# Sixteen of the up projection's column pairs in seven block products instead of fourteen, one block's split through an accumulating DMA, and smaller raw loads

## The chip, the core and the metric

The kernel runs on one NeuronCore of a Trainium2 chip. The metric is device time in microseconds of one execution. A core has a matrix engine (TensorE; the profile lists its multiplications as PE and its weight loads as PEld), three engines for elementwise work (VectorE as DVE, ScalarE as ACT, GpSimd as POOL) and SyncE (SP), which here only starts DMAs. Each engine works off its own queue in order and waits on semaphores for the others. Operands lie in SBUF, products land in PSUM.

## The reference, cut to what matters

One encoder layer on 512 positions of width 1024, all in float32. The change lies in its feed-forward part alone:

```python
h = rmsnorm(x, ffn_pre_norm[l])
up = causal_dwconv(h @ w_ffn_up[l], ffn_conv_w[l], ffn_conv_b[l])
f_gate, f_val = jnp.split(up, 2, axis=-1)
f = (jax.nn.gelu(f_gate, approximate=True) * f_val) @ w_ffn_down[l]
x = x + rmsnorm(f, ffn_post_norm[l])
```

`w_ffn_up` is 1024 x 6144: 3072 gate columns and 3072 value columns. Before it stand an SSD mixer and an RG-LRU mixer with their projections, after it the down projection; both stay as they are.

## The kernel before, in words

**Two-part operands.** Every float32 operand of a large product is split in two parts, `hi` (a cast by ACT) and `lo` (the source minus `hi`, by DVE), and each product is three matmuls: hi by hi, hi by lo, lo by hi.

**Pairs.** The up projection works on 24 pairs `n` (`NF`), each of 128 gate columns and the 128 value columns that belong to them. A pair's weights are a 2 x 2 grid of blocks `a11`, `a12`, `a21`, `a22`: the first digit is gate (1) or value (2), the second is the half of the 1024 rows; each block is 128 partitions x 512 numbers, 256 KB. Pairs 0 and 1 go whole (`up_product`). The others, from `PLAIN` = 2, go through the loop near the end of the kernel, which walks over the *slots* of a pair: one slot is one block's product.

**Eight or seven.** `eight(n, old)` (L1050) multiplies all four blocks with all 512 positions: 4 slots of 12 matmuls over 512 columns. `seven(n, old)` (L1018) splits the positions in halves too and uses a Strassen-like scheme with sums of blocks `s1` to `s4` and of activations: 6 slots in `ORDER` = a11, s2, s4, s3, a12, s1, each 12 matmuls over 256 columns (`block_product`), and a seventh product, `a22` by the fourth activation sum, which is left to the next pair (`last_product(old)`). `seven_of[n]` says which; of pairs 4 to 23, every third is an eight, which makes 14 sevens and 6 eights; pairs 2 and 3 are eights too.

**What else a pair does.** `gate_part(old)` and `value_part(old)` are the causal convolutions of the pair before (one ACT pass and two DVE passes each, L226), `gelu_part(old)` the GELU by ACT; `value_part` ends with gate times value (L866). A seven adds its products on DVE: L1031 and L1044 to L1046 in its own slots, L1005 in `value_part` once `last_product` is through. L1046 reads the half bank into which `last_product` goes on to accumulate, so `last_product` has to wait for it; the product of `a12` has to wait for L1031 likewise.

**Splits ahead.** At the end of each slot `w_split` (L955) splits the block that is used five slots later. ACT writes `hi`, DVE `lo` (L952). For a seven it also makes `s2` = `s1` + `a11` (L965, in the turn of a11) and `s4` = `s2` + `a12` (L968, in the turn of s2); with `s3` it splits `a22` as well, into a tile that the profile calls `a`. For an eight it splits a11 with a12 and a21 with a22, 1024 wide.

**Loads.** `pair_load(n + 2)` in slot 0 of pair n has SP load the whole 1 MB of pair n + 2 into one of two buffers (called `H` in the profile, L926). It must wait until pair n's blocks have been read. `pair_sums(n + 2)` then loads the first term of `s1` and of `s3` (L940, SP) and adds the second by an accumulating DMA from POOL (L942), into tiles called `raw` and `third`.

**Order.** PE and ACT keep the order in which the program is written (`InOrder`). The order of DVE, of SP and of POOL is set by the framework's scheduler when the program is built.

Of the kernel before, what the change touches and what calls it, by code (L numbers as in the profile page):

```python
# [8 lines left out]
F32 = mybir.dt.float32  # L9
# [3 lines left out]
ALU = mybir.AluOpType  # L13

P = 128
D = 1024
# [6 lines left out]
NF = FF // P  # L23
EPS = 1e-6
DT_SLAB = 1
UP_SLAB = 77
# [30 lines left out]
def block_kernel(ctx: ExitStack, tc, x, slabs, wgate, pc, rows, out):  # L57
    nc = tc.nc
    V, A, PE = (InOrder(tc, e) for e in (nc.vector, nc.scalar, nc.tensor))
    G = nc.gpsimd  # L60
# [9 lines left out]
    def ps():  # L70
        return psum.tile([P, S], F32, tag="ps", name="ps")
# [16 lines left out]
    def mm3(acc, lhi, llo, rhi, rlo, start, stop):  # L88
        mm(acc, lhi, rhi, start, False)
        mm(acc, lhi, rlo, False, False)  # L90
        mm(acc, llo, rhi, False, stop)
# [57 lines left out]
    def load_slab():  # L149
        i = stream["load"]  # L150
        if i < end[0]:
            raws[i] = wts.tile([P, D], F32, tag="raw", name="raw")
            nc.sync.dma_start(out=raws[i], in_=slabs[i])
            stream["load"] += 1
# [707 lines left out]
    def f_gate(gt):  # L862
        A.activation(gt, gt, AF.Gelu_apprx_tanh)
# [26 lines left out]
    def h_split(m):  # L890
        t = lru8(F32R).rearrange("p k (two t) -> p k two t", two=2)
        comb[m] = t[:, :, 0, :], t[:, :, 1, :]
        split(*comb[m], tsum[m])
# [4 lines left out]
    def block_product(out, w, b, start=False):  # L898

        for k in range(HK):  # L900
            c = slice(k * P, (k + 1) * P)
            for e, (u, v) in enumerate(((0, 0), (0, 1), (1, 0))):
                PE.matmul(out, lhsT=w[u][:, c], rhs=b[v][:, k, :], start=start and k == e == 0,
                          stop=k == HK - 1 and e == 2, skip_group_check=not start)

    seven_of = [False] * 4 + [i % 3 != 2 for i in range(NF - 4)] + [False]
    ORDER = "a11", "s2", "s4", "s3", "a12", "s1"
    blocks = [(n, q) for n in range(PLAIN, NF + 1)  # L910
              for q in (ORDER if seven_of[n] else ("a11", "a12", "a21", "a22"))]
# [3 lines left out]
    blk, room, spare = {}, {}, []  # L915
# [3 lines left out]
    def drawn(n, i, h):  # L919
        return slabs[UP_SLAB + 2 * n + i, :, h * S:(h + 1) * S]  # L920

    def pair_load(n):
        if n > NF:
            return
        raw = pairs[:, n % 2, :]
        nc.sync.dma_start(out=raw.rearrange("p (i c) -> p i c", i=2),  # L926
                          in_=slabs[UP_SLAB + 2 * n:UP_SLAB + 2 * n + 2].rearrange("i p c -> p i c"))
        blk[n] = {q: raw[:, e * S:(e + 1) * S] for e, q in enumerate(("a11", "a12", "a21", "a22"))}
        blk[n]["raw"] = raw

    def pair_sums(n):

        if n > NF or not seven_of[n]:
            return
        b, i = blk[n], turn_of[n]
        b["s1"] = place("raw", i % 3 - 1) if i % 3 else third
        b["s3"] = place("raw", 2 + i % 2)
        adds = ("s1", (1, 0), (1, 1)), ("s3", (0, 0), (1, 0))
        for q, one, two in adds:
            nc.sync.dma_start(out=b[q], in_=drawn(n, *one))  # L940
        for q, one, two in adds:
            G.dma_start(out=b[q], in_=drawn(n, *two), accum_op=ALU.add)  # L942

    def place(kind, i):

        key = kind, i // 2
        if key not in room:
            room[key] = wts.tile([P, D], F32 if kind == "raw" else F32R, tag=kind, name=kind)
        return room[key][:, i % 2 * S:(i % 2 + 1) * S]

    def low(lo, src, hi):
        V.tensor_sub(lo, src, hi.bitcast(F32))  # L952

    def w_split(g):

        if g >= len(blocks):
            return
        n, q = blocks[g]
        b, i = blk[n], g % RING
        both = [place(kind, i) for kind in ("whi", "wlo")]  # L960
        b["w" + q] = both
        if seven_of[n]:
            if q == "a11":
                b["s2"] = place("raw", 4)
                V.tensor_add(b["s2"], b["s1"], b["a11"])  # L965
            elif q == "s2":
                b["s4"] = place("raw", 5)
                V.tensor_add(b["s4"], b["s2"], b["a12"])  # L968
            A.copy(both[0], b[q])
            low(both[1], b[q], both[0])  # L970
            if q == "s3":
                if not spare:
                    spare.append(work.tile([P, 2, 2, S], F32R, tag="M", name="a22", bufs=1))
                b["wa22"] = [spare[0][:, n % 2, e, :] for e in range(2)]
                A.copy(b["wa22"][0], b["a22"])
                low(b["wa22"][1], b["a22"], b["wa22"][0])
        elif q in ("a12", "a22"):
            hi, lo = (room[kind, i // 2] for kind in ("whi", "wlo"))
            src = b["raw"][:, 0:D] if q == "a12" else b["raw"][:, D:2 * D]
            A.copy(hi, src)  # L980
            low(lo, src, hi)
            if n == NF:
                splits[DOWN_SLAB + (q == "a22")] = hi, lo
# [7 lines left out]
    def gate_part(n):  # L991
        p = pr[n]
        p["g"] = conv(p["oa"], pcs[:, C_FCW + 3 * n:C_FCW + 3 * n + 3], C_FCB + n, 3)

    def gelu_part(n):
        f_gate(pr[n]["g"])

    def last_product(n):
        if seven_of[n]:
            block_product(pr[n]["z"][:, T1], blk[n]["wa22"], comb[3])  # L1000

    def value_part(n):
        p = pr.pop(n)
        if seven_of[n]:
            V.tensor_add(p["ob"][:, T0], p["u2"], p["z"][:, T1])  # L1005
            w = negw[:, 3 * n:3 * n + 3]
        else:
            w = pcs[:, C_FCW + 3 * (NF + n):C_FCW + 3 * (NF + n) + 3]
        vt = conv(p["ob"], w, C_FCB + NF + n, 3)
        f_done(n, p["g"], vt)  # L1010
# [38 lines left out]
    def eight(n, old):  # L1049
        p = pr.setdefault(n, {})  # L1050
        for e, o in enumerate(("oa", "ob")):
            p[o] = acc = ps()
            for h in range(2):
                w = blk[n]["wa%d%d" % (e + 1, h + 1)]
                for k in range(HK):
                    c = slice(k * P, (k + 1) * P)
                    mm3(acc, w[0][:, c], w[1][:, c], h2T[0][:, HK * h + k, :],
                        h2T[1][:, HK * h + k, :], h == k == 0, h == 1 and k == HK - 1)
                if old:
                    if e == h == 0:  # L1060
                        gate_part(old)
                    elif e == 0:
                        gelu_part(old)
                        last_product(old)
                    elif h == 0:
                        value_part(old)
                yield

# [15 lines left out]
    def f_split(i):  # L1084
        split(*f_parts(i), f_tile(i))


    for i in range(PLAIN):
        acc = up_product()
        if i == 0:  # L1090
            pair_load(PLAIN)
            pair_load(PLAIN + 1)
        gt = conv(acc, pcs[:, C_FCW + 3 * i:C_FCW + 3 * i + 3], C_FCB + i, 3)
        if i == 0:
            w_split(0)
            w_split(1)
            for m in range(4):
                h_sum(m)
        else:
            for g in range(2, RING - 1):  # L1100
                w_split(g)
            h_split(1)
            h_split(2)
        acc = up_product()
        vt = conv(acc, pcs[:, C_FCW + 3 * (NF + i):C_FCW + 3 * (NF + i) + 3], C_FCB + NF + i, 3)
        f_gate(gt)
        f_done(i, gt, vt)
# [3 lines left out]
    for n in range(PLAIN, NF):  # L1111
        for slot, _ in enumerate((seven if seven_of[n] else eight)(n, old)):
            w_split(g + RING - 1)
            g += 1
            if slot == 0:
                pair_load(n + 2)
                pair_sums(n + 2)
            if n == PLAIN and slot in (1, 2):
                h_split(3 * (slot - 1))
            if n < NF - 1:  # L1120
                continue
            if slot == 2:
                stream.update(load=DOWN_SLAB + 2, split=DOWN_SLAB + 2, use=DOWN_SLAB)
                end[0] = slabs.shape[0]
                load_slab()
            elif slot == 3:
                f_split(0)
                f_split(1)
            elif slot == 5:
                f_split(2)  # L1130
                f_split(3)
        old = n
# [100 lines left out]
```

## Time and profile before

| | us |
|---|---|
| median of 3 runs | 880.71 (878.99 to 883.2) |
| profiled execution, own time | 882.06 |
| its span, first to last instruction | 880.4 |
| PE busy in the span | 864.7 (98%) |
| DVE busy | 587.4 (67%) |
| ACT busy | 433.6 (49%) |
| POOL busy | 28.4 (3%) |
| granted TensorE clock, mean | 0.996 |

1.66 us of the profiled execution's time lie outside its span. "Busy" counts time in which an instruction of the engine was under way; instructions of one engine overlap at their ends, so what an instruction costs its queue is the distance between the start of one and the next, and not its duration. A line such as `[0.85 <-DVE tmp L1046]` says that the engine stood idle for 0.85 us before that instruction and that it was released by DVE's instruction of line 1046.

### The profile page before, as it was taken

Reading aid. Unit: us, or ns where it says so; the run is one execution under the profiler, and the core shown is the slowest. Engines: PE = TensorE matmul, PEld = TensorE weight load, DVE = VectorE, ACT = ScalarE, POOL = GpSimd, SP = SyncE. Lnnn points to the kernel's source line nnn. Section 1 sums busy time; section 2 is a strip of 40 time slices with the busy share of each in tenths; the row PEclk is TensorE's granted clock in tenths of the full one; section 3 lists DMA queues with packets and bytes.
Section 4 is the critical chain, followed back from the end, with each engine's and each line's share of the span. In section 5 each row is a group of like instructions: output and inputs, shape, how many; then the busy total and the mean of one; then the engine's idle time right before and its main releaser. Section 6 shows DMA issues by size and latency. Waiting matters only on the chain.

```text
span 880.4 us, 11591 instructions
## 1 busy us (share of the span) xinstructions
PE 864.7 (98%) x4554; PEld 739.7 (84%) x4554; DVE 587.4 (67%) x909; ACT 433.6 (49%) x714; POOL 28.4 (3%) x44
## 2 busy tenths in 40 slices
PE   7999999999999999999999999999999999999996
PEld 6888887888878888888888989889999899888885
DVE  6777657987875553444466797878978898743225
ACT  6444545578574443322365565445545556633222
POOL 0000000000000000000000101011011000000000
PEclk9999999999999999999999999999999999999999
DMA  6242223222334422222251837466556543422212
GB/s 225 96 146 96 96 94 110 90 84 79 119 103 174 154 96 96 87 99 101 97 191 25 212 127 195 126 180 170 165 144 181 156 127 113 144 96 95 96 48 96
DMA packets 36007, 108.47 MB, mean 123 GB/s; under 512 B 3632, under 2 KB 6896, under 8 KB 35440
## 3 DMA queue, kind: packets, MB, share of 16 engines
q1 hardware_dynamic: 30864, 99.34, 32.7%
q0 software_dynamic: 5088, 8.39, 5.7%
q8 instruction: 35, 0.57, 0.2%
q14 instruction: 20, 0.16, 0.1%
HBM read 103.49 MB, written 2.13 MB: 120 GB/s over the span
## 4 chain that ended last, share of the span: by engine, by line
PE 75%; DVE 11%; DMA 7%; ACT 5%; issue 2%; SPq 0%; DVEq 0%; ACTq 0%
PE ps L53 75%; DMA H<-slabs 5%; DVE wlo L952 2%; DVE tmp L226 2%; ACT whi L53 1%; DVE wlo L183 1%; ACT L L53 1%; DVE L L644 1%; DMA raw<-slabs 1%; ACT tmp L53 1%; DVE tmp L662 1%; DVE raw L965 0%; DMA wg<-wgate 0%; DVE L L638 0%; ACT junk L247 0%
## 5 line engine op out<-in xcount | busy, mean ns | idle before, releaser
L53 PE MATMUL ps<-H,whi 128*128 128x512 f32 x720 | 224.8, 395 | 0.4 <-DVE H L53 0.4
L183 DVE TENSOR_TENSOR wlo<-raw,whi 128x1024 fp32r<-128x1024 f32 x93 | 113.6, 1223 | 117.3 <-ACT whi L53 115.0
L53 ACT CAST whi<-raw 128x1024 fp32r<-128x1024 f32 (+1 forms) x144 | 127.5, 891 | 100.2 <-PE ps L53 96.6
L53 PE MATMUL ps<-C,whi 128*128 128x256 f32 (+1 forms) x656 | 166.5, 335 | 0.1
L53 PEld LDWEIGHTS ps<-H,whi 128*128 128x128 f32 x720 | 134.3, 188 | 30.3 <-issue 2.4
L53 PE MATMUL ps<-H,wlo 128*128 128x512 f32 x352 | 137.5, 391 | 0.4 <-DVE wlo L183 0.4
L53 PEld LDWEIGHTS ps<-C,whi 128*128 128x128 f32 x656 | 112.0, 190 | 12.6 <-DVE quad L1031 0.3
L53 PE MATMUL ps<-C,wlo 128*128 128x512 f32 (+1 forms) x360 | 122.2, 339 | 0.0
L53 PE MATMUL ps<-L,whi 128*128 128x256 f32 (+1 forms) x400 | 87.2, 300 | 0.0
L53 PE MATMUL ps<-whi,H 128*128 128x512 f32 x256 | 81.5, 394 | 0.0
L226 DVE SCALAR_TENSOR_TENSOR tmp<-ps,pcs,tmp 128x511 f32<-128x511 f32 (+2 forms) x100 | 74.5, 745 | 8.1 <-ACT tmp L53 7.2
L53 PEld LDWEIGHTS ps<-H,wlo 128*128 128x128 f32 x352 | 66.2, 188 | 15.3 <-DVE wlo L183 1.2
L53 PEld LDWEIGHTS ps<-C,wlo 128*128 128x128 f32 x360 | 68.3, 190 | 7.6
L53 PEld LDWEIGHTS ps<-L,whi 128*128 128x128 f32 x400 | 64.4, 191 | 2.5
L53 PEld LDWEIGHTS ps<-whi,H 128*128 128x128 f32 x256 | 48.1, 188 | 10.4 <-issue 0.5
L53 ACT ACTIVATE tmp<-tmp 128x512 f32<-128x512 f32 x36 | 22.7, 632 | 55.3 <-DVE tmp L226 55.3
L53 PE MATMUL ps<-wlo,H 128*128 128x512 f32 x128 | 49.8, 389 | 0.0
L952 DVE TENSOR_TENSOR wlo<-H,whi 128x512 fp32r<-128x512 f32 (+1 forms) x46 | 41.1, 894 | 9.7 <-ACT whi L53 9.6
L53 PE MATMUL ps<-L,wlo 128*128 128x256 f32 x168 | 47.5, 283 | 0.0
L53 ACT ACTIVATE tmp<-ps,halfb 128x512 f32<-128x512 f32 x32 | 21.5, 687 | 49.6 <-PE ps L53 49.6
L53 ACT ACTIVATE tmp<-ps,pcs 128x512 f32<-128x512 f32 x40 | 31.0, 776 | 27.9 <-PE ps L53 27.9
L53 PE MATMUL ps<-Y,whi 128*128 128x512 f32 x128 | 40.5, 397 | 0.2 <-DVE Y L200 0.2
(207 smaller groups left out, 1315.3 us busy)
## 6 DMA issues: line engine op xcount, KB each, us to landing
raw<-slabs SPq DMA_DIRECT2D x103, 512.0 KB, 3.2
H<-slabs SPq DMA_DIRECT2D x23, 1024.0 KB, 5.4
raw<-slabs SPq DMA_DIRECT2D x23, 256.0 KB, 3.8
raw<-slabs POOLq DMA_DIRECT2D x23, 256.0 KB, 6.5
quad<-x SPq DMA_DIRECT2D x8, 512.0 KB, 4.2
M<-acsD SPq DMA_DIRECT2D x4, 1024.0 KB, 4.6
out<-tmp SPq DMA_DIRECT2D x8, 256.0 KB, 2.0
third<-slabs SPq DMA_DIRECT2D x5, 256.0 KB, 6.3
```

The costliest lines, as they stand in the source:

```text
L53: return lambda *args, **kw: self.tc.keep_in_program_order(op(*args, **kw))
L183: V.tensor_sub(*late.pop(0))
L226: V.scalar_tensor_tensor(out=t[:, d:], in0=acc[:, :S - d], scalar=w[:, taps - 1 - d:taps - d], in1=t[:, d:], op0=ALU.mult, op1=ALU.add)
L644: V.tensor_tensor_scan(out=qq[:, e, :], data0=aa[:, e, :], data1=uu[:, e, :], initial=0.0, op0=ALU.mult, op1=ALU.add)
L662: V.tensor_mul(gl, gl, hs[i // 4][:, i % 4, :])
L952: V.tensor_sub(lo, src, hi.bitcast(F32))
```

## The change

More pairs go as sevens: 16 of pairs 4 to 23, with eights at 7, 12, 17 and 22, so that up to four sevens follow each other where it was two. The raw load is cut: of a seven, a11 and a12 come first (512 KB), then the terms of the sums, then a22 alone (256 KB); a21 is no longer loaded raw, and a22 takes the place of a21 or a22 in turn, so that it does not fall on the place that the pair two before it used. An eight's load comes in two halves. `s2` and `s4` are each made one turn later, just ahead of their own split. The low part of a22 is no longer made by DVE: ACT writes -hi into it, and a DMA from POOL adds a22. And in an eight, `last_product(old)` and `value_part(old)` move one slot back.

```diff
-    seven_of = [False] * 4 + [i % 3 != 2 for i in range(NF - 4)] + [False]
+    seven_of = [False] * 4 + [i % 5 != 3 for i in range(NF - 4)] + [False]
@@ pair_load
-        nc.sync.dma_start(out=raw.rearrange("p (i c) -> p i c", i=2),
-                          in_=slabs[UP_SLAB + 2 * n:UP_SLAB + 2 * n + 2].rearrange("i p c -> p i c"))
+        nc.sync.dma_start(out=raw[:, 0:D], in_=slabs[UP_SLAB + 2 * n])
         blk[n] = {q: raw[:, e * S:(e + 1) * S] for e, q in enumerate(("a11", "a12", "a21", "a22"))}
         blk[n]["raw"] = raw
+        if seven_of[n]:
+            blk[n]["a22"] = blk[n][("a21", "a22")[n // 2 % 2]]
+            pair_sums(n)
+            nc.sync.dma_start(out=blk[n]["a22"], in_=drawn(n, 1, 1))
+        else:
+            nc.sync.dma_start(out=raw[:, D:], in_=slabs[UP_SLAB + 2 * n + 1])
@@ w_split
-            if q == "a11":
+            if q == "s2":
                 b["s2"] = place("raw", 4)
                 V.tensor_add(b["s2"], b["s1"], b["a11"])
-            elif q == "s2":
+            elif q == "s4":
                 b["s4"] = place("raw", 5)
                 V.tensor_add(b["s4"], b["s2"], b["a12"])
             A.copy(both[0], b[q])
@@ w_split, with s3
-                A.copy(b["wa22"][0], b["a22"])
-                low(b["wa22"][1], b["a22"], b["wa22"][0])
+
+                hi, lo = b["wa22"]
+                A.copy(hi, b["a22"])
+                A.mul(lo, hi.bitcast(F32), -1.0)
+                G.dma_start(out=lo.bitcast(F32), in_=b["a22"], accum_op=ALU.add)
@@ eight
                     elif e == 0:
                         gelu_part(old)
+                    elif h == 0:
                         last_product(old)
-                    elif h == 0:
+                    else:
                         value_part(old)
@@ the loop over pairs, slot 0
                 pair_load(n + 2)
-                pair_sums(n + 2)
```

## Rows read from the trace of the kernel before

**Rows 1.** Page, part 1: busy time, share of the span and instructions of each engine

```profile
PE 864.7 (98%) x4554; PEld 739.7 (84%) x4554; DVE 587.4 (67%) x909; ACT 433.6 (49%) x714; POOL 28.4 (3%) x44
```

**Rows 2.** Page, part 4: chain that ended last, by engine

```profile
PE 75%; DVE 11%; DMA 7%; ACT 5%; issue 2%; SPq 0%; DVEq 0%; ACTq 0%
```

**Rows 3.** Busy time by stretch, pairs 6 to 23; each stretch starts with a matmul

```profile
core 0: us, PE busy (x) PEld busy (x) DVE busy (x) ACT busy (x) POOL busy (x), PEclk, DMA share, GB/s
550.55:564.04 13.49, 12.64 (x62) 10.38 (x61) 10.41 (x18) 4.70 (x10) 0.85 (x1) 1.00 0.37 104
...
615.49:627.85 12.36, 12.36 (x62) 10.45 (x61) 11.59 (x20) 7.66 (x13) 0.84 (x1) 1.00 0.54 141
...
691.53:710.25 18.72, 18.72 (x158) 18.71 (x157) 16.41 (x29) 10.34 (x20) 2.58 (x3) 1.00 0.71 194
...
sum 190.75, PE 187.88 PEld 174.77 DVE 162.32 ACT 100.58 POOL 17.06; mean PE 15.66 PEld 14.56 DVE 13.53 ACT 8.38 POOL 1.42
```

**Rows 4.** Waits of PEld, 531 to 742: us in total, times, longest

```profile
PEld ps L53 <- DVE tmp L1046: 4.4, 4, 1.5
PEld ps L53 <- DVE quad L1031: 0.3, 1, 0.3
```

**Rows 5.** Timeline of PE inside pair 6, an eight: start, us, instructions, idle before

```profile
555.79 0.39 PE L53 MATMUL ps<-C,wlo 128*128 128x512 f32 x1
557.03 1.70 PE L53 MATMUL ps<-L,a 128*128 128x256 f32 x12 [0.85 <-DVE tmp L1046]
```

**Rows 6.** Waits of DVE, 531 to 742

```profile
DVE raw L965 <- DMA H<-slabs: 14.8, 9, 2.7
DVE wlo L952 <- ACT whi L53: 12.3, 15, 1.4
```

**Rows 7.** Timeline of DVE where seven 19 ends and seven 20 begins

```profile
699.77 0.68 DVE L952 TENSOR_TENSOR wlo<-raw,whi 128x512 fp32r<-128x512 f32 x1
700.37 0.75 DVE L226 SCALAR_TENSOR_TENSOR tmp<-ps,pcs,tmp 128x510 f32<-128x510 f32 x1
701.03 0.68 DVE L952 TENSOR_TENSOR a<-H,a 128x512 fp32r<-128x512 f32 x1
701.63 0.69 DVE L866 TENSOR_TENSOR Y<-tmp 128x512 f32<-128x512 f32 x1
702.23 0.42 DVE L1044 TENSOR_TENSOR quad<-quad,ps 128x256 f32<-128x256 f32 x1
702.57 0.69 DVE L952 TENSOR_TENSOR wlo<-H,whi 128x512 fp32r<-128x512 f32 x1
...
703.50 0.42 DVE L1046 TENSOR_TENSOR tmp<-ps,quad 128x256 f32<-128x256 f32 x1
704.53 0.75 DVE L226 SCALAR_TENSOR_TENSOR tmp<-tmp,pcs 128x511 f32<-128x511 f32 x1 [0.61 <-ACT tmp L53]
```

**Rows 8.** Timeline of DVE around the start of pair 15, an eight

```profile
643.50 1.22 DVE L952 TENSOR_TENSOR wlo<-H,whi 128x1024 fp32r<-128x1024 f32 x1 [1.36 <-ACT whi L53]
644.65 0.41 DVE L1005 TENSOR_TENSOR tmp<-quad,ps 128x256 f32<-128x256 f32 x1
646.57 0.69 DVE L965 TENSOR_TENSOR raw<-raw,H 128x512 f32<-128x512 f32 x1 [1.51 <-DMA H<-slabs]
```

**Rows 9.** Page, part 6: DMA issues, count, KB each, median us to landing

```profile
raw<-slabs SPq DMA_DIRECT2D x103, 512.0 KB, 3.2
H<-slabs SPq DMA_DIRECT2D x23, 1024.0 KB, 5.4
...
raw<-slabs POOLq DMA_DIRECT2D x23, 256.0 KB, 6.5
```

**Rows 10.** Timeline of ACT in the same stretch as rows 7

```profile
699.48 0.62 ACT L53 CAST a<-H 128x512 fp32r<-128x512 f32 x1
700.00 0.36 ACT L53 COPY tmp<-ps 128x256 f32<-128x256 f32 x1
```

**Rows 11.** Groups by line on POOL, 550 to 742: busy us, mean ns | idle before

```profile
L942 POOL DMA_DIRECT2D raw<-slabs x17 | 14.5, 872 | 122.2 <-DMA raw<-slabs 121.4 <-issue 0.7
```

## The prediction

> **What bounds the kernel now.** I read the page's busy times first: PE is busy for 98% of the span, the next engine, DVE, for 67% [rows 1]. The chain that ended last agrees: 75% of it is PE, 11% DVE, 7% DMA [rows 2]. So time can only be won by giving PE less to do, or by closing the gaps in which it waits. The change touches the up projection's pairs alone, so I cut that stage into stretches of an eight, or of the sevens between two eights [rows 3]. Two kinds come out clean. An eight with the left-over product of the seven before it takes 12.36 us with PE busy throughout. Two sevens (13 products, since the last one is left over) take 18.72 us, or 1.44 us a product, 0.120 us a matmul. The eight alone is thus 12.36 - 1.44 = 10.92 us (0.2275 us a matmul), a seven is 7 x 1.44 = 10.08 us. The clock stands at 1.00 in all stretches, the upper of its two levels, 2.4 GHz.
>
> Six eights and six couples would take 6 x 12.36 + 6 x 18.72 = 186.48 us; they took 190.75 [rows 3]. The difference, **4.27 us, is all that PE loses in these pairs**. The waits say where: weight loads waited 4.4 us in four places for L1046 and 0.3 us for L1031 [rows 4]. The timeline shows one of the four: in eight 6, after the first half of its products, PE stands for 0.85 us until DVE is through with L1046, and the left-over product can start [rows 5].
>
> Why is DVE late there? It is not only busy; it waits: 14.8 us for raw loads at L965 and 12.3 us for ACT's casts at L952 [rows 6]. At L965 it stands 1.51 us in one instance, with L1044 to L1046 queued behind it [rows 8].
>
> **Part 1, two eights become sevens.** PE saves 2 x (10.92 - 10.08) = **1.68 us** [rows 3], on the path, since PE is the path. By the row a matmul costs its columns at 2.4 GHz and about 13 ns more (0.120 against 0.1067, 0.2275 against 0.2133). The Trainium skill (TensorE: Matmul & The Clock Gate, Wait — 56ns, not 53.3ns?) gives only about 2.5 ns more per matmul; by that the two pairs would save 2.4 us (estimate), but here 13 ns is measured, and a seven has 84 matmuls against 48, so the row decides.
>
> **Part 2, what DVE has to do.** Distances between starts are the cost: 0.60 us for a 512-wide subtraction, 0.66 for a convolution pass, 0.34 for a 256-wide addition [rows 7], 1.15 for a 1024-wide subtraction [rows 8]. A seven before: six block splits 3.60, a22 0.60, s2 and s4 1.20, four convolution passes 2.64, five additions 1.70, the last product 0.60: 10.34 us, more than the 10.08 that PE takes. After: 9.74. An eight: 2 x 1.15 + 2.64 + 0.60 = 5.54 of 10.92. Over pairs 4 to 23 DVE has 14 x 10.34 + 6 x 5.54 = 178.0 us before and 16 x 9.74 + 4 x 5.54 = 178.0 after: no change in sum, but it no longer falls behind by work alone while sevens follow each other. This is worth nothing in itself; it is what the next parts live on.
>
> **Part 3, last product one slot later in an eight.** L1046 had 5.46 us after the seven's end (half the eight, 10.92 / 2); it gets three quarters, 8.19 us. The longest of these waits was 1.5 us [rows 4], so 2.73 us more covers all four. Gain: up to 4.4 us of the waits; counted in the gap total, at most 4.27. The place where it can come back: `value_part` moves with it, so L1005, the last two passes and L866 (0.34 + 1.32 + 0.60 = 2.26 us of DVE) come 2.73 us later and end in the next seven's first slots, where L1031 must be done before the product of a12, 5.76 us in. That wait is at 0.3 us already [rows 4].
>
> **Part 4, smaller loads, s2 and s4 a turn later.** H landed in 5.4 us, 512 KB pieces in 3.2 [rows 9]; the addition s2 is due one slot (1.44 us) later. Together 3.6 us of slack against waits of at most 2.7 us [rows 6]: I expect nearly all of the 14.8 us of DVE idle time at L965 to go. PE gets none of that directly; it is DVE's lateness that shrinks. The price: ACT's cast of s2 now follows s2's addition directly, then comes the `lo` on DVE. The trace of before has no such chain. Lower bound 0, if the scheduler puts other DVE work between; upper bound two ACT casts of 0.52 us [rows 10] per seven, during which DVE stands. I take 0.2 us, nearer to 0, since DVE has some ten other instructions a pair to put there.
>
> **Part 5, a22's low part by DMA.** ACT gains one more pass of 0.52 us per seven [rows 10]; it is busy 10.34 of 18.72 us [rows 3], so that hides; if ACT were full, it would be 16 x 0.52 = 8.3 us. POOL gets a third issue per seven, 0.87 us [rows 11]; it is idle nearly always. Landing takes 6.5 us like the other accumulating DMAs [rows 9]. Cast, pass, issue and landing are 0.52 + 0.52 + 0.87 + 6.5 = 8.4 us from slot 4 of the pair before; the product is due after slot 3 of the pair after, in sevens 1.44 + 10.08 + 4 x 1.44 = 17.3 us later. The margin of 8.9 us can be lost behind a sum whose load is late on POOL's queue, where this DMA then stands too; I count 0, and rival C has the other end. The bytes moved per seven are the same 2 MB, at a DMA share of 0.71 [rows 3], so transfers stay hidden.
>
> **Part 6, four sevens in a row.** A seven then has 9.74 us of work, 0.61 us of waiting for ACT's convolution pass [rows 7] and 0.2 from part 4: 10.55 us against 10.08. So DVE falls behind by about 0.5 us per seven. At the end of the first of a run L1046 was through at 703.92 [rows 7], 3.75 us after the seven's end at 691.53 + 6 x 1.44 = 700.17 [rows 3]; the fourth would be at 5.2 us, under the 5.76 that a seven leaves and the 8.19 that an eight leaves. L1031 is tighter. I put 1.2 us for the stage (three runs of four, 0.2 us in the third and fourth); bounds 0 and 4.27, the gap total of now.
>
> **Sum.** 1.68 + 4.27 - 1.2 = **4.75 us** off the profiled execution's 882.06 (880.4 of span and 1.66 around it): 877.31. The median of the runs shown is 1.35 us below that execution, so 880.71 - 4.75 = **876.0 us**, with all gaps closed 874.8.
>
> **Rivals.** A: the gaps move. DVE is still late, PE now waits at L1031 and in the later `last_product`; only the 1.68 us are won: 879.0. For it: DVE's total work is unchanged and L1031 is at its limit already. Against: 14.8 us of DVE waiting go. B, slower: **DVE becomes the bound** through the chain add, cast, subtract of s2 and s4. Should DVE stand for both casts, a seven costs it 9.74 + 0.61 + 1.04 = 11.39 us, 1.31 over PE's time. Four of them are 5.2 us late. An eight gives back 10.92 - 5.54 - 1.36 [rows 8] = 4.0. That alone would cost 1.2 us in each of four runs; with the casts late too, because ACT keeps its order and waits for DVE itself (another 0.6 us a seven, an estimate after the 0.61 of [rows 7]), it is 3.6 us a run and 14.4 in all. In place of the gaps of now that gives 880.7 - 1.7 - 4.3 + 14.4 = 889. It decides from 10.08 + 4.0 / 4 = 11.1 us of DVE time a seven. Against it: the scheduler may fill these holes with other DVE work. C: the change does not do what it says: POOL's third DMA comes late behind a sum's load, last products wait for it in a few places. With four waits of 1.1 us, which is what those for L1046 cost, the gap total stays and the time is 879, as in A; PE's waits on the DMA into `a` would tell the two apart.
>
> **How the numbers follow.** A measurement of this kernel can tell about 0.5%, 4.4 us, from no change; the forecast of 4.7 lies just beyond. Chances: the forecast 0.52, A and C together 0.32, B 0.16. Of the forecast's cases a few end within 4.4 us, and of A's a few beyond it: faster 0.50, within 0.5% 0.36, slower 0.14. The range goes from all gaps closed, less the spread of the runs below their median (874.8 - 1.3 = 873.5), to A with part of B: 884.0; most of B and a little below are left out.
>
> **What would show it.** Stretches of sevens at 10.08 us a pair and eights at 12.36 with no rest; no wait of PE for L1046 within eights; L965's wait on the raw load gone; the group a<-H on DVE gone and a third POOL DMA in its place; waits for L1031 short. Wrong would be it if PE waits for DVE in the third and fourth sevens of a run, if DVE's busy share rises over 95% there, or if PE waits on the DMA into `a`.

## The result, and the profile after

The changed kernel takes **891.56 us** (median of 6 runs, 889.65 to 893.09), the kernel before 880.12 in the same runs (878.47 to 883.20): a ratio of 1.0125, 95% interval 1.0102 to 1.0148. That is **11.4 us slower**, where 4.7 us faster was forecast, and above the range. The profiled execution took 891.87 us, its span 890.1.

The page's busy times and the chain by engine, as in [rows 1] and [rows 2]:

```profile
PE 865.8 (97%) x4626; PEld 743.2 (83%) x4626; DVE 587.5 (66%) x917; ACT 448.3 (50%) x744; POOL 45.8 (5%) x64
...
PE 73%; DVE 11%; DMA 7%; ACT 5%; issue 2%; SPq 1%; POOL 0%; DVEq 0%; POOLq 0%; ACTq 0%
```

PE is busy hardly longer and DVE just as long (587.5 against 587.4 us): what grew is time in which PE stands. From the first matmul of pair 4 to the first of the down projection it took 218.3 us, before 209.5. These 8.9 us are most of the 9.8 by which the two profiled executions differ. The untouched start of the kernel differs by 1.1 us besides, as it does from execution to execution (its 301st matmul starts from 67.2 to 69.7 us into the span in the profiles of this study), and what comes after is nearly equal (138.8 us after, 139.0 before).

The stretches of eights and of four sevens, as in [rows 3]: eight 7, sevens 8 to 11, eight 12, sevens 13 to 16, eight 17, sevens 18 to 21, eight 22.

```profile
core 0: us, PE busy (x) PEld busy (x) DVE busy (x) ACT busy (x) POOL busy (x), PEclk, DMA share, GB/s
561.74:576.14 14.40, 12.67 (x63) 10.34 (x61) 9.14 (x15) 4.10 (x9) 0.85 (x1) 1.00 0.53 154
576.14:617.84 41.70, 39.41 (x326) 39.02 (x325) 36.49 (x65) 27.28 (x51) 9.47 (x11) 1.00 0.71 167
617.84:634.84 17.00, 14.22 (x62) 11.50 (x61) 10.70 (x18) 5.99 (x11) 0.85 (x1) 0.90 0.51 150
634.84:674.68 39.84, 39.41 (x325) 39.01 (x324) 34.85 (x62) 26.22 (x48) 9.43 (x11) 1.00 0.74 176
674.68:689.17 14.49, 12.67 (x62) 10.34 (x61) 9.14 (x15) 4.83 (x10) 0.87 (x1) 1.00 0.58 172
689.17:730.30 41.13, 39.43 (x326) 39.02 (x325) 37.58 (x67) 27.01 (x50) 7.71 (x9) 1.00 0.69 173
730.30:742.66 12.36, 12.36 (x62) 10.45 (x61) 9.14 (x16) 7.63 (x14) 0.86 (x1) 1.00 0.43 148
sum 180.92, PE 170.18 PEld 159.68 DVE 147.03 ACT 103.06 POOL 30.04; mean PE 24.31 PEld 22.81 DVE 21.00 ACT 14.72 POOL 4.29
```

Without a gap an eight with its left-over product takes 12.36 us and four sevens 27 x 1.44 = 38.88: 166.08 us in all. They took 180.92. The gaps are **14.84 us**, against 4.27 before; more than half of them (2.04 + 4.64 + 2.13) lie in the eights, the rest in the first and third sevens of a run. A gap here is all time beyond these prices; of the 4.64 us in eight 12 some 1.6 are matmuls at a lower granted clock (0.90 over the stretch; see the last section). Who was waited for, as in [rows 4] and [rows 6], PEld's and DVE's waits from 531 to 752 (L957 is the low part, L1039 the former L1031, L970 the addition of s2):

```profile
PEld ps L53 <- DVE wlo L957: 7.6, 3, 3.2
PEld ps L53 <- DVE quad L1039: 3.9, 3, 1.8
...
DVE raw L970 <- DMA H<-slabs: 19.5, 5, 6.4
DVE wlo L957 <- ACT whi L53: 11.4, 16, 1.6
```

The waits for the former L1046 are gone. But PE now waits for low parts, which it did not do in these pairs before, and DVE stands at the addition of s2 for a raw load five times and up to 6.4 us, not nine times and up to 2.7. The loads have become smaller (H lands in 4.6 us at 512 KB, 5.4 at 1 MB before), and yet they come later. SP's own waits in the same stretch say why (L932 is the load of a22, L934 that of an eight's second half):

```profile
SPq L932 <- DMA a<-H: 37.9, 7, 8.8
SPq L934 <- DMA a<-H: 25.3, 4, 7.1
```

SP stood for 63 us behind the new accumulating DMAs. One instance, at eight 12, in five timelines (SP, ACT, POOL, DVE, PE; start, us, instructions, idle before):

```profile
606.49 0.33 SPq L934 DMA_DIRECT2D H<-slabs  x1
606.90 0.38 SPq L926 DMA_DIRECT2D H<-slabs  x1
607.39 1.83 SPq L945 DMA_DIRECT2D raw<-slabs  x2
618.08 0.33 SPq L932 DMA_DIRECT2D H<-slabs  x1
618.50 0.38 SPq L926 DMA_DIRECT2D H<-slabs  x1
...
620.25 0.37 SPq L926 DMA_DIRECT2D H<-slabs  x1
...
608.54 0.63 ACT L53 ACTIVATE a<-a 128x512 fp32r<-128x512 f32 x1
...
612.34 0.86 POOL L947 DMA_DIRECT2D raw<-slabs  x1 [9.36 <-DMA raw<-slabs]
612.91 1.18 POOL L984 DMA_DIRECT2D a<-H  x1
...
615.45 1.23 DVE L957 TENSOR_TENSOR wlo<-H,whi 128x1024 fp32r<-128x1024 f32 x1 [1.37 <-ACT whi L53]
616.59 0.42 DVE L1013 TENSOR_TENSOR tmp<-quad,ps 128x256 f32<-128x256 f32 x1
623.43 0.69 DVE L970 TENSOR_TENSOR raw<-raw,H 128x512 f32<-128x512 f32 x1 [6.42 <-DMA H<-slabs]
624.15 0.69 DVE L973 TENSOR_TENSOR raw<-raw,H 128x512 f32<-128x512 f32 x1
624.76 0.74 DVE L226 SCALAR_TENSOR_TENSOR tmp<-tmp,negw 128x511 f32<-128x511 f32 x1
625.42 1.22 DVE L957 TENSOR_TENSOR wlo<-H,whi 128x1024 fp32r<-128x1024 f32 x1
...
623.30 0.61 PE L53 MATMUL ps<-C,whi 128*128 128x512 f32 x2
626.70 0.54 PE L53 MATMUL ps<-C,wlo 128*128 128x512 f32 x1 [2.78 <-DVE wlo L957]
```

At 609.3 SP comes to a load of a22 (L932) and waits until 618.08 for POOL's DMA of 612.91 to land. That DMA reads a22 of pair 11, and the load is to overwrite the place: the next pair that uses it is **pair 15**. Behind it in SP's queue, and so stuck, are the raw loads of pairs **13 and 14** (618.50 and 620.25). The framework's scheduler sets SP's order, and it had put a load four pairs ahead in front of two that were due at once. DVE then stands 6.42 us at the addition of s2 of pair 13, with the low part of eight 12's second half (625.42) behind it, and for this PE waits in the middle of eight 12. It is the same at eights 7 and 17, where DVE stands 6.11 and 5.46 us.

The place is held so long for two reasons. ACT had written -hi at 609.17 (608.54 + 0.63), but POOL issued the DMA only at 612.91: its queue too is worked off in order, and ahead stood the addition into a sum (612.34), for whose first term POOL had waited. That is 3.7 us; the landing took another 5.2.

### The profile page after: what moved, and what is told of

Same layout as the page of the kernel before. It is cut to its first block, busy times and chain, and to the rows that moved or that the text cites. A ratio compares the mean times of both kernels' runs of the same rounds, so it can differ in the third digit from the quotient of the medians.

```text
span 890.1 us, 11927 instructions
## 1 busy us (share of the span) xinstructions
PE 865.8 (97%) x4626; PEld 743.2 (83%) x4626; DVE 587.5 (66%) x917; ACT 448.3 (50%) x744; POOL 45.8 (5%) x64
## 3 DMA queue, kind: packets, MB, share of 16 engines
HBM read 101.39 MB, written 2.13 MB: 116 GB/s over the span
## 4 chain that ended last, share of the span: by engine, by line
PE 73%; DVE 11%; DMA 7%; ACT 5%; issue 2%; SPq 1%; POOL 0%; DVEq 0%; POOLq 0%; ACTq 0%
PE ps L53 73%; DMA raw<-slabs 3%; DVE tmp L226 2%; DMA a<-H 2%; DVE wlo L957 2%; DMA H<-slabs 2%; ACT tmp L53 1%; ACT whi L53 1%; DVE wlo L183 1%; ACT L L53 1%; DVE L L644 1%; DVE tmp L662 0%; DVE L L638 0%; DVE raw L970 0%; DMA wg<-wgate 0%
## 5 line engine op out<-in xcount | busy, mean ns | idle before, releaser
L53 ACT CAST whi<-raw 128x1024 fp32r<-128x1024 f32 (+1 forms) x151 | 131.0, 878 | 100.0 <-PE ps L53 98.0
L53 PE MATMUL ps<-C,whi 128*128 128x256 f32 (+1 forms) x640 | 157.3, 329 | 4.4 <-DVE quad L1039 4.3
L53 PE MATMUL ps<-C,wlo 128*128 128x256 f32 (+1 forms) x352 | 117.4, 334 | 6.3 <-DVE wlo L957 6.3
L53 PEld LDWEIGHTS ps<-C,whi 128*128 128x128 f32 x640 | 108.2, 191 | 15.6 <-DVE quad L1039 3.9
L53 PE MATMUL ps<-L,whi 128*128 128x256 f32 (+1 forms) x448 | 96.1, 298 | 0.0
L53 PEld LDWEIGHTS ps<-C,wlo 128*128 128x128 f32 x352 | 67.2, 191 | 14.0 <-DVE wlo L957 7.6
L226 DVE SCALAR_TENSOR_TENSOR tmp<-ps,pcs,tmp 128x511 f32<-128x511 f32 (+2 forms) x92 | 68.6, 746 | 9.7 <-ACT tmp L53 8.8
L53 PEld LDWEIGHTS ps<-L,whi 128*128 128x128 f32 x448 | 71.9, 191 | 2.5
L53 PEld LDWEIGHTS ps<-whi,H 128*128 128x128 f32 x256 | 48.1, 188 | 10.4 <-issue 0.5
L53 PE MATMUL ps<-L,wlo 128*128 128x256 f32 x192 | 54.3, 283 | 0.0
L947 POOL DMA_DIRECT2D raw<-slabs x26 | 24.1, 951 | 553.5 <-DMA raw<-slabs 544.1
L957 DVE TENSOR_TENSOR wlo<-raw,whi 128x512 fp32r<-128x512 f32 x58 | 38.6, 687 | 6.2 <-ACT whi L53 6.2
```

What stands on the lines that cost most here:

```text
L53: return lambda *args, **kw: self.tc.keep_in_program_order(op(*args, **kw))
L226: V.scalar_tensor_tensor(out=t[:, d:], in0=acc[:, :S - d], scalar=w[:, taps - 1 - d:taps - d], in1=t[:, d:], op0=ALU.mult, op1=ALU.add)
```

## The experiments

Two theories stood at the start. **Q**: the wait of SP's queue makes the loss. **D**: DVE is the bound, the prediction's rival B, through four sevens in a row and the chain addition, cast, subtraction. Medians are given; the kernel before, in the same chip's runs, was 881.6 beside e1 to e4, 880.9 beside e5 to e8, 879.5 beside e9 to e12 and 879.7 beside e13 and e14. "Stage" is the time from the first matmul of pair 4 to the first of the down projection in the profiled execution (before 209.5, after 218.3). It is of one execution, which can lie some us from the median of its kernel: 5.0 above it in e7, 4.0 below it in e9. To pin a DMA is to have the scheduler keep it in the order in which it is written.

**e1: pin the load of a22 behind its pair's raw load.**

```diff
@@ pair_load, of the kernel after
-        nc.sync.dma_start(out=raw[:, 0:D], in_=slabs[UP_SLAB + 2 * n])
...
         if seven_of[n]:
             blk[n]["a22"] = blk[n][("a21", "a22")[n // 2 % 2]]
             pair_sums(n)
-            nc.sync.dma_start(out=blk[n]["a22"], in_=drawn(n, 1, 1))
-        else:
-            nc.sync.dma_start(out=raw[:, D:], in_=slabs[UP_SLAB + 2 * n + 1])
+        nc.sync.dma_start(out=raw[:, 0:D], in_=slabs[UP_SLAB + 2 * n])
+        if seven_of[n]:
+            last = nc.sync.dma_start(out=blk[n]["a22"], in_=drawn(n, 1, 1))
+        else:
+            last = nc.sync.dma_start(out=raw[:, D:], in_=slabs[UP_SLAB + 2 * n + 1])
+        tc.keep_in_program_order(last)
```

> The kernel after, with one thing changed: in pair_load the terms of the sums are issued first, then the load of a11 and a12, and the load of a22 (for an eight, of a21 and a22) is pinned behind it on SP's queue, so that no a22 load can stand ahead of the raw load of an earlier pair. Theory Q (queue): in the kernel after, the a22 load of a pair four further on stands in SP's queue ahead of the raw loads of the next two sevens and waits there for the accumulating DMA that reads its place; the raw loads come late, DVE (L970) and ACT stand, PE waits in the eights. Q expects 877 to 881 us, DVE's waits at L970 down from 19.5 us to under 5, and PE's waits for the low part in eights (7.6 us) gone. Rival D (DVE is the bound, by four sevens in a row and the chain addition, cast, subtraction): 891 us as after, with PE waiting for DVE in the third and fourth sevens.

Measured: **875.45 us**, ratio to before 0.9927 (0.9909 to 0.9945), stage 204.6. Q holds (the time is even 1.6 us under its span), and D falls: DVE's work is the same as in the kernel after, with the same four sevens in a row. DVE's waits at the addition of s2 (now L972) fell less than expected, to 8.9 us; that was enough. The same stretches as above, the worst two, the next two and the sum, and DVE's waits:

```profile
559.18:572.11 12.93, 12.66 (x63) 10.38 (x62) 11.37 (x19) 7.25 (x12) 1.65 (x2) 1.00 0.53 133
572.11:611.51 39.40, 39.08 (x325) 38.90 (x324) 35.44 (x63) 24.89 (x47) 8.67 (x11) 1.00 0.79 191
611.51:623.88 12.37, 12.37 (x62) 10.46 (x61) 10.52 (x18) 8.00 (x14) 1.70 (x2) 1.00 0.66 169
623.88:662.75 38.87, 38.87 (x325) 38.87 (x324) 35.45 (x63) 24.54 (x46) 8.59 (x10) 1.00 0.78 194
...
sum 167.18, PE 166.59 PEld 158.39 DVE 147.57 ACT 104.35 POOL 30.05; mean PE 23.80 PEld 22.63 DVE 21.08 ACT 14.91 POOL 4.29
...
DVE raw L972 <- DMA H<-slabs: 8.9, 5, 3.8
```

Gaps are 167.18 - 166.08 = 1.10 us, where the prediction had put 1.2. This version is faster than both kernels.

**e2: a22's low part by DVE again** (`low(b["wa22"][1], b["a22"], b["wa22"][0])` in place of ACT's pass and the DMA, all else as after).

> The kernel after, with a22's low part made by DVE as before (no ACT pass, no accumulating DMA); everything else as after. Theory Q: the places of a22 come free with DVE's subtraction instead of with a DMA that lands some 5 us after POOL has issued it; the loads queued behind get out earlier and POOL's sums no longer stand behind a DMA that waits for ACT: 878 to 884 us. Rival D: DVE has 16 x 0.60 = 9.6 us more to do, so 893 us or more.

Measured: 878.46 us, ratio 0.9967 (0.9945 to 0.9988). The waits of SP for `a<-H` are gone with the DMA (it waits 8.5 us for DVE's subtraction in their place), DVE's at L970 are 8.7 us, and 16 subtractions more for DVE cost less than the queue did. Q again.

**e3: the kernel before with 16 sevens alone** (the line of `seven_of`).

> The kernel before with 16 sevens and nothing else of the change (line of seven_of alone). Theory Q: two pairs at 0.84 us saved, the gaps of before at L1046 stay in four eights instead of six: 877 to 881 us. Rival D: DVE has 10.34 us a seven against 10.08 of PE, over runs of four: 886 us or more.

Measured: 882.82 us, ratio 1.0007 (0.9986 to 1.0028), a little above Q's span and far from D's. In the profiled execution, one of the fastest of the ten (879.0 us), the stage took 207.8 us, 1.7 less than before, with gaps as large (4.25 us, before 4.28) but in another place: PE waited for L1031 in the third seven of each run of four, and nowhere for L1046.

```profile
PE ps L53 <- DVE quad L1031: 3.6, 3, 1.7
```

That is D's picture on a small scale. Over the runs the gain of 1.7 us does not show.

**e4: the kernel before with `last_product` and `value_part` a slot later in an eight, alone.**

> The kernel before with last_product and value_part one slot later in an eight, and nothing else. By the prediction's part 3 the waits of PE for L1046 go (4.4 us before) and little comes back: 876 to 877.5 us. If the gaps only move (to L1031 in the next seven, since value_part comes later), 879 to 880.

Measured: **891.17 us**, ratio 1.0103 (1.0071 to 1.0135), stage 215.9. Both expectations miss. The waits for L1046 did go, as forecast, but those for L1031 rose from 0.3 us to 9.2 (PEld's waits, against [rows 4]):

```profile
PEld ps L53 <- DVE quad L1031: 9.2, 5, 2.8
PEld ps L53 <- DVE tmp L1046: 0.2, 1, 0.2
```

**e5: e1 without the pin** (the same order of writing, SP's order left to the scheduler: the last line of e1's diff is left out).

> As e1_a22_load_behind_raw, without the pin: the sums are written first, but SP's order is left to the scheduler, which puts the a22 loads where the kernel after has them. Theory Q: the pin alone made the difference, so this is 889 to 893 us, with DVE waiting some 19 us at L970. Rival: the order in which the loads are written (sums ahead of raw) made it: 875 to 878 us.

Measured: **891.6 us**, ratio 1.011 (1.0073 to 1.0147), stage 220.9. The pin alone is the difference. SP's wait for the accumulating DMAs and DVE's wait for loads are back:

```profile
SPq L933 <- DMA a<-H: 40.9, 7, 9.2
...
DVE raw L971 <- DMA H<-slabs: 21.8, 4, 7.3
```

**e6: the kernel after with the a22 load alone pinned**, behind the load of s3.

```diff
-            nc.sync.dma_start(out=blk[n]["a22"], in_=drawn(n, 1, 1))
+            tc.keep_in_program_order(nc.sync.dma_start(out=blk[n]["a22"], in_=drawn(n, 1, 1)))
```

> The kernel after, with a22's load alone pinned behind the load of s3 of the same pair (the raw loads are not touched, and an eight's loads neither). s3's place comes free only with the split two sevens earlier, so that no a22 load gets ahead of raw loads. Theory Q: 875 to 880 us; a little above e1, since an eight's second half can still stand ahead of its first. Rival (the wait of the eight's second load for the accumulating DMA is what counts, not the a22 loads): 886 to 891 us.

Measured: 876.76 us, ratio 0.9956 (0.9931 to 0.9981), stage 204.6. One call around one DMA takes back the whole loss. In an eight SP still waits 24.4 us in four places for the accumulating DMA (L934); no loss from this shows in the time.

**e7: e1 with a22's low part by DVE.**

> As e1_a22_load_behind_raw, with a22's low part made by DVE as before. It tells what the split by ACT and an accumulating DMA is worth once SP's order is mended. By the prediction's part 2 DVE has 10.34 us a seven in place of 9.74, more than PE's 10.08, in runs of four: 878 to 881 us, PE waiting for DVE in third and fourth sevens. Theory Q alone (DVE was late only because it stood for loads): 875 to 877 us, as e1.

Measured: 876.02 us, ratio 0.9934 (0.9908 to 0.9961). By the medians the split by ACT and DMA is worth nothing that can be told, once SP's order is right. Whether DVE keeps up with 10.34 us a seven differs from execution to execution: five of the eight took 875.4 to 876.2 us, but the profiled one is the slowest (881.07, stage 209.6), and in it PE waited 2.7 us for L1038, the former L1031, in the third sevens of the three runs.

**e8: e4 with s2 and s4 a turn later.**

> The kernel before with two parts of the change: last_product and value_part a slot later in an eight (which alone gave 891), and s2 and s4 a turn later. If the loss of e4 came from DVE standing at L965 for the raw load (23 us) while value_part's passes and L1031 wait behind, the later addition takes part of it: DVE's waits at L965 under 10 us, PE's for L1031 under 4 us (9.2 in e4), 880 to 885 us. If value_part's place alone made it: 889 to 892.

Measured: 891.77 us, ratio 1.0107 (1.0068 to 1.0147). This is in the second span: the later turn took nothing away. DVE waited 23.9 us at L965, PE 9.7 for L1031.

**e9: e4 with the raw load in parts** (pinned as in e1; s2, s4 and a22's low part as before).

> The kernel before (14 sevens, s2 and s4 and a22's low part as before) with two parts of the change: last_product and value_part a slot later in an eight, which alone gave 891, and the raw load in parts (a11 and a12 first, a22 alone at its own place behind it, pinned on SP as in e1). In e4 and e8 DVE stood some 23 us at L965 for the 1 MB load, and L1031 came late behind. If the load is the cause, DVE's waits at L965 fall under 10 us, PE's waits for L1031 under 2 us, and the time is 876 to 879. If the place of value_part is the cause, 888 to 892 stays.

Measured: 887.12 us (883.13 to 887.65), ratio 1.0066 (1.0042 to 1.0090): between the two, and near the second. The profiled execution was the fastest one; in it no wait for L1031 was left, DVE waited 10.2 us for loads, and PE lost 3.9 us in one place, in eight 21, where it stood 2.0 us for a low part and then ran at a lower granted clock. What the slower executions lost is not known.

**e10: e1 with 14 sevens** (`i % 3 != 2`).

> As e1_a22_load_behind_raw with 14 sevens instead of 16 (every third pair an eight, as before). It tells what the two more sevens are worth: by the prediction's part 1 1.7 us, so 877.1 us (876.5 to 877.8) against e1's 875.45. If four sevens in a row cost DVE as much as they save PE, 875 to 876.

Measured: 879.55 us, ratio 0.9994 (0.9967 to 1.0021), above what was expected. The two more sevens are worth 4.1 us between the medians, and 2.5 us in the stage of the profiled executions (207.1 against 204.6), of which 0.8 are gaps (1.9 against 1.1) and 1.7 products, at the prices of [rows 3]. With 14 sevens no gain over the kernel before can be told.

**e11: the kernel before with the raw load in parts alone** (pinned).

> The kernel before with the raw load in parts alone (pinned as in e1; last_product where it was, 14 sevens). It tells whether the gaps of before at L1046 come from DVE standing for the 1 MB load: if so, DVE is on time, those waits (4.4 us) fall under 1.5 us, and it is 877 to 878.5 us. If DVE's own work makes them, 880 to 882, as before.

Measured: 879.55 us, ratio 1.0010 (0.9993 to 1.0028). The profiled execution has the expected picture, 0.8 us of waits for the former L1046 and a stage of 205.7 us, 3.8 less than before; the median does not move. That the gaps of before come from DVE standing for the load is borne out by the trace, and not by the time. The stage of before that is compared here is of an execution of 882.06 us, 2.6 above the median of its kernel beside e11, so that much of the 3.8 us may be that execution's.

e9 differs from e11 in the later place of `last_product` and `value_part` alone, and took 7.6 us more in the same runs, with the load in parts in both. So the late load is not the whole of the loss in e4. e10 has the later place too, and besides the later s2 and s4 and a22's low part by DMA, and took no more than e11. Which of these two makes the later place harmless is not shown.

**e12: e1 with 18 sevens** (`i % 10 != 3`, up to nine in a row).

> As e1_a22_load_behind_raw with 18 sevens (eights at 7 and 17 only, up to nine sevens in a row). PE saves another 2 x 0.84 = 1.7 us: 873.8 us, if DVE with 9.74 us of work a seven keeps up. By the prediction's part 6 DVE falls behind by 0.5 us a seven, 2 to 3 us over nine sevens more than the ring of splits and the slack of L1039 take: 875 to 880 us, PE waiting for L1039 from the fourth seven on.

Measured: 884.39 us, ratio 1.0049 (1.0030 to 1.0067). This lies above the span that was expected for a late DVE (875 to 880). PE waits in the third to the sixth seven of the run of nine and in the fourth and fifth of the last run, and not in the seventh to ninth; PE's waits, L1041 being the former L1031:

```profile
PE ps L53 <- DVE quad L1041: 8.0, 6, 1.8
...
DVE raw L972 <- DMA H<-slabs: 14.2, 9, 4.6
```

DVE also stood for raw loads longer than in e1 (14.2 against 8.9 us), so its work is not shown to be all that makes it late.

**e13: e1 with `last_product` and `value_part` in an eight where they were before.**

> As e1_a22_load_behind_raw, with last_product and value_part in an eight where they were before. If the prediction's part 3 holds once the loads come in time, L1046's successor makes PE wait in the four eights again: 877 to 880 us, against e1's 875.45. If DVE is on time anyway (e11 had hardly any wait for it), 875 to 876.5; if the later place costs as it did in e4, 870 to 874.

Measured: 875.59 us, ratio 0.9947 (0.9929 to 0.9964), stage 205.4 (on another chip, as e14). In this kernel the later place is worth nothing that can be told.

**e14: e1 with s2 and s4 a turn earlier, as before.**

> As e1_a22_load_behind_raw, with s2 and s4 added a turn earlier, as before. By the prediction's part 4 DVE then stands longer at the addition of s2 for the raw load (8.9 us in e1, 12 to 20 expected here): 877 to 880 us. If the turn makes no difference, as in e8: 875 to 876.5.

Measured: 876.52 us, ratio 0.9972 (0.9955 to 0.9989), stage 205.4. At most a small gain of the later turn: 1.1 us between the medians, 0.8 in the stage, and the ratios' intervals just do not touch; against e13, in the same runs, it is 0.9 us, and the intervals overlap. DVE's waits for loads are 10.4 us, 8.9 in e1.

## Why the prediction was wrong, step by step

**What bounds the kernel** was read rightly: the stage is PE's, and gaps are what counts. Part 2 was right too in that DVE's work did not change (587.5 and 587.4 us), nor did it make the loss.

**The step that failed is the transfers**, in parts 4 and 5. Part 5 asked of the new DMA whether its result comes in time for the left-over product; it did, with no wait of PE for it in the kernel after. What the step left out is the other end: **the DMA also reads**, and until it has landed, the place of a22 can't be loaded again. Before, DVE's subtraction freed it. And the load that waits for the place stands in SP's queue, which is worked off in order, with the next pairs' raw loads behind. Part 5 had named POOL's queue and put 0 for it (it was 3.7 us in the instance above); SP's, into which part 4 puts more loads, was not walked through. Nothing in the trace of before said where the scheduler would put a load of a22, but its freedom was known, since SP's order is not written in the program. The bound to write down would have been that a load of a free place may stand ahead of anything. Its price is measured by e1 against e5, 875.45 to 891.6: **16 us**.

So part 4's gain did not come: the loads got smaller and DVE's waits for them rose from 14.8 to 19.5 us. With SP's order mended they fall to 8.9, not to nearly nothing. One term was also too small: the 3.2 us for 512 KB are of another group of loads in [rows 9], and H at 512 KB landed in 4.6 us after and in 5.1 in e1.

**Part 1** was sized rightly: 1.68 us forecast; e1's stretches without a gap take 12.37 us for an eight with the left-over product and 38.87 for four sevens, so 10.93 an eight, 10.08 a seven and 1.7 us for two pairs. (The 1.7 us that e3 and e10 give are no test of their own, since their gaps are counted from the same prices.) By the Trainium skill's 2.5 ns per matmul (TensorE: Matmul & The Clock Gate, Wait — 56ns, not 53.3ns?) it would have been 2.4 us (estimate); the row was the better guide.

**Part 3** was wrong in size on its far side. The waits for L1046 went, as said; the place where they might come back was named too, L1031, but taken at 0.3 us where e4 shows 9.2. DVE stood 23.1 us at L965 in e4, and the passes that were moved had to come after. But e9 against e11 shows that most of the loss stays when the load comes in parts, so this reason is argued and not shown to be the whole. In e13 against e1 the later place is worth nothing.

**Part 6** holds within its bounds: the stretches have gaps of 1.10 us in e1 (1.2 forecast). That the two agree so well is in part luck: about half of the 1.10 lies in eight 7, for a low part, the rest in the first run of four alone. The place that part 6 named, L1031 in the third seven, is where PE waits in e3, e7 and e12; that DVE's work alone makes it late there is not shown, since in e12 it also stands longer for loads.

**The rivals.** B gave 889 us, near what came, but by a mechanism that e1 rules out: DVE has the same work there, with the same chain of addition, cast and subtraction, and DVE's waits for casts did not grow in the kernel after (11.4 us, before 12.3). Its sum also counts four runs of four sevens, where there are three, as part 6 has it. C was right in its subject, the new DMA comes late behind others, but looked for PE's waits on the DMA into `a`, of which there were none. With the queue mended, the sum of the forecast comes out: 876.0 us forecast, 875.45 and 876.76 measured in e1 and e6; 4.75 us were to go, and e1's stage is 4.9 shorter. Not each part does: part 3 gives nothing that shows in e13's time, and the loads in parts alone leave 0.8 us of PE's waits in e11.

**Left open**: what e9's slower executions lost (its profiled one, the fastest, has the stage of before, 209.3 us, and took 883.13 us, where the profiled one of before took 882.06); what makes the later place of `last_product` and `value_part` cost 7.6 us in e9 and nothing in e1; and why e7's executions differ by 5.6 us.

## What to carry to other kernels

A DMA that takes over an engine's step also takes over the holding of that step's source: ask which load wants the place next, and what stands behind that load in its queue. Where a scheduler orders a DMA queue, a load into a place that comes free early can be put ahead of loads that are due now; pin it behind them, as one call did here for 15 us (891.6 after, 876.8 in e6). And a step moved later to escape a wait can bring a longer wait elsewhere: the move alone cost 10 us here (e4), and gave nothing in the fastest version (e13 against e1).

## What the runs showed of the hardware

After the longest gap of the changed kernel PE's granted clock fell: PE had stood 2.78 us before 626.70, in a stretch before that with the clock at 1.00, and the next 3.74 us ran at 0.54, near the lower level of 1.2 GHz, then at 1.00 again:

```profile
623.30:626.70 3.40, 0.62 (x4) 0.19 (x2) 3.24 (x5) 0.62 (x1) 0.85 (x1) 1.00 0.27 64
626.70:630.44 3.74, 3.74 (x9) 2.93 (x10) 3.73 (x8) 1.32 (x2) 0.00 (x0) 0.54 0.67 179
```

Eight matmuls of 512 columns took 0.43 us each from start to start there in place of 0.23: 1.6 us more on top of the gap. The length of the gap alone does not tell whether the clock falls. After the gaps of 1.73 and 1.82 us in eights 7 and 17 it stayed at 1.00, and in e5 it did so after the longest gap of all, 3.63 us before 624.73. But in e7 it fell after 1.88 us of standing (before 705.00) and in e9 after 2.01 (before 709.91), each time a little after PE had started again. The stretches that follow, of e5, e7 and e9:

```profile
624.73:628.50 3.77, 3.77 (x22) 3.31 (x23) 3.76 (x8) 1.33 (x2) 0.00 (x0) 1.00 0.74 182
...
706.40:709.00 2.60, 2.60 (x14) 2.60 (x14) 2.60 (x6) 1.80 (x4) 0.00 (x0) 0.50 0.09 14
...
711.20:714.80 3.60, 3.60 (x10) 2.83 (x9) 3.56 (x6) 1.56 (x3) 0.00 (x0) 0.53 0.33 126
```

What else decides is left open.
